# The credit for GpSimd is taken out of the rule that chooses engines during attention

## The chip, the cores and the metric

The kernel runs on one core of a Trainium2 chip. The metric is the device time of one execution in microseconds; lower is better. The core's engines are named as in the profile: PE is TensorE's matmul (PEld its weight load), DVE is VectorE, ACT is ScalarE, POOL is GpSimd, SP is SyncE, which here issues the DMAs.

## What is computed

Two layers of a diffusion backbone over 1024 latent tokens and 256 context tokens, all in float32. Each layer normalises and modulates its input, projects it, and feeds three branches: a gated convolution of width 31, windowed attention, and gated linear attention in chunks of 64. Their gated outputs are concatenated and go through one output projection. The part that matters here is the attention's softmax, cut from the reference:

```python
s_loc = jnp.where(mn, jnp.einsum('bqhgd,bkhd->bhgqk', qn, kn).astype(F32), NEG_INF)
s_ctx = jnp.einsum('bqhgd,bchd->bhgqc', qn, kc).astype(F32)
p = jax.nn.softmax(jnp.concatenate([s_sink, s_ctx, s_loc], axis=-1), axis=-1)
...
return (jnp.einsum('bhgqc,bchd->bqhgd', p_ctx, vc)
        + jnp.einsum('bhgqk,bkhd->bqhgd', p_loc, vn))
```

## The kernel before, in words

**Scheduling.** The program is written by generators ("lanes") that run while the kernel is built. A clock model in the kernel (class `Model`) keeps a clock for each engine and adds a price for every instruction that is written. `loop` always continues the lane of the highest priority whose condition the model holds fulfilled. So the model fixes, before anything runs, the order in which each engine gets its instructions; on the chip each engine works through its queue in that order.

**Choosing an engine.** Small elementwise steps can go to more than one engine. `pick` takes the option that ends first by the model: the later of the engine's clock and PE's clock, plus the price, minus a credit from the table `LEAN`. The table has two entries; the second holds while `self.rsv` is set, that is from the start of a layer's attention (`attn_start`) until the scores of its last block are written (`phase_bc`).

```python
c = self.nc.clock
lean = LEAN[1 if self.rsv else 0]
min(opts, key=lambda o: max(c[o[0]], c["pe"]) + o[1] - lean.get(o[0], 0))[2]()
```

GpSimd is an option in three helpers: `scale` (a tile times one number per row; DVE, POOL or ACT), `sub` (DVE or POOL) and `add` (DVE or POOL). `scale` multiplies the attention's probabilities by the inverse of their sum. `sub` makes the low half of every tensor that `split` cuts into a rounded high half and a rest, for the products in three parts: weights, queries, keys and the input of the output projection. `add` adds the residual behind the output projection. The prices that the model uses for n elements per row in `scale` are these:

```python
self.pick(("dve", 130 + n / 1.92, ...),
          ("pool", 110 + 1.1 * n, ...),
          *([("act", 135 + n / 1.4, ...)] if f == 1.0 else []))
```

**Attention.** A unit is one block of 128 queries with 4 heads; layer 0 has 20 units, layer 1 has 16. For each head `u_score` lets PE write the scores into a pair of PSUM banks (two pairs exist), `u_head` masks them and takes the row maximum in one DVE instruction (shown as CUSTOM_DVE_ANT_0; only then is the bank pair free) and ACT exponentiates them. When the four heads are done, `u_run` takes the reciprocal on DVE, scales four tiles P (640 wide, 512 or 256 in some blocks), and PE transposes them by products with the identity (`idr`); `u_ev` copies each transpose out on ACT or DVE, and `u_pv` multiplies it with the values. At most two units hold P tiles at one time. `kv_prep` and `q_prep` load and split the keys and queries of later blocks.

**What runs beside it.** The output projection (`out_proj`, `out_tiles`, `out_mm`: 128x256 products of WS or H with H or SM) has the lowest priority but the program itself and fills PE between the units. In layer 0 the gate projections and the modulation of layer 1 do so too.

Of the kernel before, what the change touches and what calls it, by code (L numbers as in the profile page):

```python
# [168 lines left out]
class Hybrid:  # L169
# [190 lines left out]
    def pick(self, *opts):  # L360
# [4 lines that stand above are left out]
# [1399 lines left out]
MODN = 2  # L1764
MODG = 1
MDC = 1
LEAN = ({}, dict(pool=800))
XG = 2000
B_GATE = [(6, 0), (7, 0), (6, 1), (7, 1), (6, 2), (7, 2)]

# [85 lines left out]
```

## Time and profile before

| | |
|---|---|
| median of 3 runs | 1326.59 us (1323.63 to 1327.82) |
| the profiled execution, its own time | 1323.65 us |
| its span, first to last instruction | 1321.9 us |
| PE busy | 1254.0 us, 95% |
| DVE, ACT, POOL busy | 838.4, 561.2, 452.9 us |

All times of views below count from the start of the profiled execution's span. Nearly every instruction carries line 43, that of a helper which issues for all engines, so instructions are told apart by their tiles: SM are small working tiles (P among them), tir small columns, ps PSUM banks, H and WS weights and inputs, U the spare region that attention uses for raw queries.

### The profile page before, as it was taken

Reading aid. Unit: us, or ns where it says so; the run is one execution under the profiler, and the core shown is the slowest. Engines: PE = TensorE matmul, PEld = TensorE weight load, DVE = VectorE, ACT = ScalarE, POOL = GpSimd, SP = SyncE. Lnnn points to the kernel's source line nnn. Section 1 sums busy time; section 2 is a strip of 40 time slices with the busy share of each in tenths; the row PEclk is TensorE's granted clock in tenths of the full one; section 3 lists DMA queues with packets and bytes.
Section 4 is the critical chain, followed back from the end, with each engine's and each line's share of the span. In section 5 each row is a group of like instructions: output and inputs, shape, how many; then the busy total and the mean of one; then the engine's idle time right before and its main releaser. Section 6 shows DMA issues by size and latency. Waiting matters only on the chain.

```text
span 1321.9 us, 24553 instructions
## 1 busy us (share of the span) xinstructions
PE 1254.0 (95%) x9518; PEld 1066.9 (81%) x9518; DVE 838.4 (63%) x1571; ACT 561.2 (42%) x1280; POOL 452.9 (34%) x609
## 2 busy tenths in 40 slices
PE   6999988999999999899999899988999999999997
PEld 3668988898887777687899879977888888788897
DVE  5745897884364463465354676898954656766554
ACT  3721341235332565466541561441245246665531
POOL 1410045674122342444230241055571334344410
PEclk9999989999999999999999999999999999999999
DMA  9453113222014323342132541114231112231012
GB/s 330 151 154 105 48 39 85 70 69 85 25 33 131 112 77 100 96 129 89 49 113 88 156 164 57 49 41 108 71 91 37 55 46 81 73 93 50 33 65 81
DMA packets 113237, 116.49 MB, mean 88 GB/s; under 512 B 38464, under 2 KB 81760, under 8 KB 113120
## 3 DMA queue, kind: packets, MB, share of 16 engines
q1 hardware_dynamic: 113120, 114.92, 28.5%
q8 instruction: 75, 1.23, 0.4%
q14 instruction: 42, 0.34, 0.1%
HBM read 95.47 MB, written 19.42 MB: 87 GB/s over the span
## 4 chain that ended last, share of the span: by engine, by line
PE 69%; DVE 8%; POOL 6%; DMA 6%; issue 5%; ACT 4%; SPq 1%; POOLq 0%; DVEq 0%; ACTq 0%
PE ps L43 69%; POOL SM L43 4%; DVE SM L43 3%; ACT SM L43 2%; DVE mix L43 2%; DMA WR<-in_w_out_dram 2%; DVE H L43 2%; DMA WR<-in_w_mod_dram 2%; POOL WR L43 1%; DMA WR<-in_w_in_dram 1%; DVE WS L43 1%; SPq L43 1%; DMA HC<-in_w_mod_dram 1%; ACT H L43 1%; ACT L43 0%
## 5 line engine op out<-in xcount | busy, mean ns | idle before, releaser
L43 PE MATMUL ps<-H,WS 128*128 128x512 f32 x1344 | 339.7, 400 | 2.9 <-DVE stat L43 1.4
L43 PEld LDWEIGHTS ps<-H,WS 128*128 128x128 f32 x1344 | 244.3, 189 | 63.8 <-issue 12.2
L43 PE MATMUL ps<-WS,H 128*128 128x256 f32 x1744 | 254.8, 291 | 0.0
L43 PEld LDWEIGHTS ps<-WS,H 128*128 128x128 f32 x1744 | 230.4, 195 | 10.0 <-issue 9.5
L43 ACT ACTIVATE SM<-ps 128x512 f32<-128x512 f32 (+2 forms) x164 | 82.7, 509 | 343.6 <-PE ps L43 289.3
L43 DVE SCALAR_TENSOR_TENSOR mix<-U,small,mix 128x1295 f32<-128x1295 f32 (+1 forms) x120 | 180.9, 1549 | 0.0
L43 PE MATMUL ps<-idr,SM 128*128 128x128 f32 (+1 forms) x1076 | 150.5, 273 | 26.2 <-POOL SM L43 16.4
L43 PEld LDWEIGHTS ps<-idr,SM 128*128 128x128 f32 (+1 forms) x1076 | 120.0, 142 | 56.0 <-POOL SM L43 22.0
L43 DVE CUSTOM_DVE_ANT_0 SM<-ps,SM,small 128x640 f32<-128x640 f32 (+2 forms) x128 | 102.7, 813 | 60.1 <-PE ps L43 53.5
L43 ACT ACTIVATE SM<-SM,stat 128x641 f32<-128x641 f32 (+2 forms) x144 | 110.7, 769 | 69.5 <-DVE stat L43 47.2
L43 POOL TENSOR_TENSOR tir<-tir,mhalf 128x1 f32<-128x1 f32 (+2 forms) x55 | 47.3, 863 | 199.2 <-DVE tir L43 192.3
L43 POOL TENSOR_TENSOR SM<-SM,SM 128x128 fp32r<-128x128 f32 (+3 forms) x59 | 60.9, 1041 | 158.7 <-ACT SM L43 107.9
L43 PE MATMUL ps<-H,H 128*128 128x256 f32 x592 | 99.0, 287 | 3.7 <-DVE H L43 2.0
L43 ACT ACTIVATE H<-ps 128x512 f32<-128x512 f32 (+1 forms) x129 | 72.7, 596 | 65.2 <-PE ps L43 63.7
L43 POOL TENSOR_SCALAR SM<-SM,tir 128x640 f32<-128x640 f32 (+2 forms) x90 | 75.8, 855 | 44.3 <-DVE tir L43 29.7
L43 PEld LDWEIGHTS ps<-H,H 128*128 128x128 f32 x592 | 83.8, 189 | 5.5 <-DVE H L43 2.2
L43 ACT ACTIVATE SM<-SM 32x128 f32<-32x128 f32 (+3 forms) x194 | 70.3, 369 | 38.3 <-DVE SM L43 30.0
L43 PE MATMUL ps<-SM,SM 128*32 128x128 f32 (+4 forms) x764 | 79.0, 285 | 5.9 <-DMA SM<-vd 3.1
L43 PE MATMUL ps<-H 128*64 128x256 f32 x548 | 72.3, 388 | 0.7 <-ACT ps L43 0.3
L43 POOL TENSOR_TENSOR SM<-SM,WR 128x256 f32<-128x256 f32 (+2 forms) x60 | 61.8, 1036 | 20.0 <-DVE SM L43 13.8
L43 DVE TENSOR_TENSOR WS<-WR,WS 128x512 fp32r<-128x512 f32 x66 | 60.7, 932 | 5.2 <-ACT WS L43 3.6
L43 PEld LDWEIGHTS ps<-SM,SM 128*64 128x64 f32 (+2 forms) x764 | 45.4, 127 | 20.0 <-ACT SM L43 6.1
(151 smaller groups left out, 1989.8 us busy)
## 6 DMA issues: line engine op xcount, KB each, us to landing
WR<-in_w_in_dram SPq DMA_DIRECT2D x80, 256.0 KB, 3.7
WR<-in_w_mod_dram SPq DMA_DIRECT2D x64, 256.0 KB, 3.2
WR<-in_w_out_dram SPq DMA_DIRECT2D x32, 256.0 KB, 3.5
SM<-vd SPq DMA_DIRECT2D x116, 64.0 KB, 2.4
x<-SM SPq DMA_DIRECT2D x20, 256.0 KB, 2.5
SM<-x SPq DMA_DIRECT2D x20, 256.0 KB, 4.3
qd<-SM SPq DMA_DIRECT2D x18, 256.0 KB, 2.2
mix<-in_x_dram SPq DMA_DIRECT2D x8, 512.0 KB, 8.3
```

Source lines behind the costliest of these rows:

```text
L43: r = getattr(self._e, op)(*a, **k)
```

## The change

The credit for GpSimd is removed from the second entry of the table. No other line differs.

```diff
-LEAN = ({}, dict(pool=800))
+LEAN = ({}, {})
```

Since the chosen engine moves the model's clocks, the written order changes with it, from the first scores of layer 0's attention to that layer's end and again in layer 1's attention; what stands ahead of each attention is almost the same. The counts over the whole program: of the 144 scalings of P, POOL had 86, DVE 40 and ACT 18; now POOL has 45, DVE 72 and ACT 27. Of the subtractions and additions 72 go from POOL to DVE. In layer 1, POOL's scalings of P fall from 34 to 26 only.

POOL, layer 0, the eighth unit: its four P tiles (SM_671 to SM_674) before the change, with a weight's low half ahead and a query's behind.

```order
L43 TENSOR_TENSOR H_0_105_495<-WR_707_5091,H_0_105_495 128x512
L43 TENSOR_SCALAR SM_671_4959<-SM_671_4959,tir 128x640
L43 TENSOR_SCALAR SM_672_4960<-SM_672_4960,tir 128x640
L43 TENSOR_SCALAR SM_673_4961<-SM_673_4961,tir 128x640
L43 TENSOR_SCALAR SM_674_4962<-SM_674_4962,tir 128x640
L43 TENSOR_TENSOR SM_719_5176<-U,SM_719_5176 128x4x64
```

DVE at the same unit after the change: its tiles are now SM_701 to SM_704, and ISA is the masking with the maximum.

```order
L43 ISA SM_704_5038,stat<-ps_67,SM_426_3819,small 128x640
L43 ISA stat 128x1
L43 CAST H_1_7_112<-ps_68 128x512
L43 CAST SM_713_5122<-U 128x4x64
L43 CAST H_0_105_495<-WR_712_5102 128x512
L43 TENSOR_TENSOR H_0_105_495<-WR_712_5102,H_0_105_495 128x512
L43 RECIPROCAL tir<-stat 128x4
L43 TENSOR_SCALAR SM_701_5035<-SM_701_5035,tir 128x640
L43 TENSOR_SCALAR SM_702_5036<-SM_702_5036,tir 128x640
L43 TENSOR_SCALAR SM_704_5038<-SM_704_5038,tir 128x640
```

Three of the four scalings now stand in DVE's queue one behind the other, and so does the weight's low half; the fourth is ACT's.

PE in layer 1 after the change, where the ninth unit begins: products of the output projection (ps_71 and ps_70), the transposes of two prepared keys (SM_1589, SM_1591), then the unit's first scores (HC).

```order
L43 MATMUL ps_71<-H_1_106_496,H_1_7_112 128x256 x2
L43 MATMUL ps_71<-H_1_106_496,SM_1580_11523 128x256
L43 MATMUL ps_68<-idr,SM_1589_11673 128x128 x4
L43 MATMUL ps_69<-idr,SM_1591_11683 128x128 x4
L43 MATMUL ps_70<-H_0_105_495,H_1_7_112 128x256 x12
L43 MATMUL ps_66<-HC_494 128x256 x2
L43 MATMUL ps_66<-HC_494 128x128 x2
```

Ahead of these scores 234 products of the output projection stand with no score between them; before the change the most between two scores of one attention was 60. The keys wait for working tiles, which the output projection holds. From the ninth unit's first score to the sixteenth's, PE had 634 products before, 288 of them of the output projection; now it has 486, with 156. DVE's own instructions there number 88 before and 89 now.

## Rows read from the trace of the kernel before

**Rows 1.** The page: the span, and busy time of each engine over it.

```profile
span 1321.9 us, 24553 instructions
...
PE 1254.0 (95%) x9518; PEld 1066.9 (81%) x9518; DVE 838.4 (63%) x1571; ACT 561.2 (42%) x1280; POOL 452.9 (34%) x609
```

**Rows 2.** Both attentions: length; busy PE, PEld, DVE, ACT, POOL; clock, DMA share, GB/s.

```profile
433.00:683.00 250.00, 240.69 (x1821) 189.38 (x1820) 131.02 (x312) 143.52 (x322) 94.09 (x174) 1.00 0.30 91
...
1073.00:1278.00 205.00, 201.32 (x1553) 172.44 (x1552) 133.06 (x288) 121.56 (x259) 85.02 (x144) 1.00 0.21 65
```

**Rows 3.** PE's waits in 433:683, by what ended them: us in total, times, longest.

```profile
PE ps L43 <- DVE H L43: 3.4, 3, 2.0
PE ps L43 <- POOL H L43: 1.7, 2, 1.0
PE ps L43 <- DVE stat L43: 0.9, 2, 0.5
PE ps L43 <- DVE SM L43: 0.8, 1, 0.8
PE ps L43 <- POOL SM L43: 0.7, 2, 0.4
```

**Rows 4.** The same in 1073:1278.

```profile
PE ps L43 <- DVE stat L43: 1.8, 3, 0.9
PE ps L43 <- POOL SM L43: 1.0, 3, 0.3
PE ps L43 <- DVE tir L43: 0.6, 1, 0.6
```

**Rows 5.** POOL's groups by shape, whole run: busy, mean ns, idle before.

```profile
L43 POOL TENSOR_SCALAR SM<-SM,tir 128x640 f32<-128x640 f32 x54 | 49.9, 937 | 15.8 <-DVE tir L43 15.7
...
L43 POOL TENSOR_TENSOR WS<-WR,WS 128x512 fp32r<-128x512 f32 x22 | 31.4, 1431 | 71.5 <-ACT WS L43 47.8 <-DVE WS L43 19.8 <-PE ps L43 3.6
```

**Rows 6.** DVE's groups by shape, whole run.

```profile
L43 DVE CUSTOM_DVE_ANT_0 SM<-ps,SM,small 128x640 f32<-128x640 f32 x96 | 83.6, 879 | 47.2 <-PE ps L43 44.1 <-POOL SM L43 1.5 <-issue 1.5
L43 DVE TENSOR_TENSOR WS<-WR,WS 128x512 fp32r<-128x512 f32 x66 | 60.7, 932 | 5.2 <-ACT WS L43 3.6
...
L43 DVE TENSOR_SCALAR SM<-SM,tir 128x640 f32<-128x640 f32 x26 | 21.7, 867 | 0.4
...
L43 DVE TENSOR_SCALAR H<-ps 128x512 f32<-128x512 f32 x24 | 16.4, 686 | 11.9 <-PE ps L43 10.5 <-ACT SM L43 1.4
L43 DVE TENSOR_TENSOR mix<-ps,mix 128x256 f32<-128x256 f32 x36 | 15.2, 422 | 42.7 <-PE ps L43 41.6 <-issue 0.9
...
L43 DVE TENSOR_TENSOR SM<-U,SM 128x256 fp32r<-128x256 f32 x6 | 3.7, 616 | 3.2 <-ACT SM L43 3.2
```

**Rows 7.** Timeline in 538:562: POOL and DVE (start, us, what, idle before).

```profile
542.20 3.13 POOL L43 TENSOR_SCALAR SM<-SM,tir 128x640 f32<-128x640 f32 x4 [0.47 <-DVE tir L43]
...
548.06 0.55 DVE L43 TENSOR_SCALAR SM<-SM,tir 128x640 f32<-128x640 f32 x1
549.77 0.56 DVE L43 CAST H<-WR 128x512 fp32r<-128x512 f32 x1 [1.16 <-DMA WR<-in_w_out_dram]
```

**Rows 8.** Timeline of PE in 542.0:550.5.

```profile
544.61 0.33 PE L43 MATMUL ps<-idr,SM 128*128 128x128 f32 x1 [0.28 <-POOL SM L43]
545.38 1.41 PE L43 MATMUL ps<-idr,SM 128*128 128x128 f32 x9 [0.44 <-POOL SM L43]
...
550.39 0.39 PE L43 MATMUL ps<-H,H 128*128 128x256 f32 x1 [2.03 <-DVE H L43]
```

**Rows 9.** Timeline in 1107:1112: DVE and POOL scale at the same time.

```profile
1108.48 1.58 DVE L43 TENSOR_SCALAR SM<-SM,tir 128x640 f32<-128x640 f32 x2
...
1108.55 2.69 POOL L43 TENSOR_SCALAR SM<-SM,tir 128x640 f32<-128x640 f32 x2 [2.66 <-DVE tir L43]
```

**Rows 10.** Busy time by stretch: ninth to sixteenth unit of layer 1, then output projection alone.

```profile
1176.00:1260.00 84.00, 83.45 (x689) 74.39 (x686) 54.90 (x117) 50.12 (x110) 35.41 (x63) 1.00 0.17 56
...
1280.00:1305.00 25.00, 25.00 (x215) 25.00 (x214) 14.41 (x27) 3.62 (x10) 1.21 (x2) 1.00 0.22 74
```

## Prediction

> **What bounds the kernel now.** I read the page first: PE is busy for 1254.0 us of a span of 1321.9 [rows 1], so no other engine can give back more than the 68 us in which PE stands still. The change is silent outside attention, so I cut the two attentions out next, layer 0 from 433 to 683 and layer 1 from 1073 to 1278 [rows 2]. The reader is to see three things there: the granted clock is 1.00, the upper level (2.4 GHz), in both; PE is busy for 240.69 of 250 and for 201.32 of 205 us, so it idles for 9.3 and 3.7 us, 13.0 together; and DVE is busy for 131.0 (52%) and 133.1 us (65%), POOL for 94.1 and 85.0. Thirteen us is therefore the most that any choice of engines can win in attention if PE's work stays the same, while a loss has no such bound.
>
> Then I asked who ends PE's idle time. In layer 0 DVE ends 3.4 + 0.9 + 0.8 = 5.1 us of the listed waits and POOL 1.7 + 0.7 = 2.4 [rows 3]; in layer 1 DVE 1.8 + 0.6 = 2.4 and POOL 1.0 [rows 4]. One of DVE's waits isn't its own: PE stood for 2.03 us before 550.39 for a weight half of DVE [rows 8], and DVE's rounding of weights there had itself waited 1.16 us for a DMA [rows 7]. I take that 2.0 off, which leaves 3.1 us in layer 0. What the change aims at is also visible: at 542.20 POOL scales four tiles of P in a row, 3.13 us [rows 7], and PE's transposes wait twice for them, 0.28 and 0.44 us [rows 8].
>
> **What the change moves, and what each part costs.** By the written order POOL loses 41 scalings of P and 72 subtractions and additions. DVE gains 32 of the scalings and all 72 others; ACT gains 9 scalings. The other moves (a few roundings and evictions between ACT and DVE) about cancel in the attentions, and I price them at nothing. PE's own work and the DMAs stay the same but for their order.
>
> *Time added to DVE.* A scaling of 640 takes 0.55 us on DVE when POOL doesn't scale beside it [rows 7] and 0.867 on average [rows 6]. The 72 others are 30 of 128 columns, 17 of 256 and 25 of 512. For the 47 narrow ones I take bounds of 0.42 (a two-input product of 256) and 0.62 (a subtraction of 256 as it now stands), for the wide ones 0.69 (a one-input copy of 512) and 0.93 (a weight's low half) [rows 6]. Low: 32 x 0.55 + 47 x 0.42 + 25 x 0.69 = 54.6 us. High: 32 x 0.87 + 47 x 0.62 + 25 x 0.93 = 80.2 us. I take 55, the low end, since POOL's work about halves: what leaves it is, as an estimate from [rows 5, 7], 41 x 0.78 + 47 x 0.8 (taken like a scaling) + 25 x 1.43 = 105 of 179 us at most. Of the moved instructions 62 are layer 0's (28 scalings, 34 others) and 42 layer 1's (4 and 38): 33 and 22 us.
>
> *(a) PE's waits for DVE grow.* DVE works in order, and the instruction that frees a pair of score banks (0.879 us) [rows 6] now stands behind up to four scalings and the low halves. I let these waits grow as DVE's busy time over its idle time. Layer 0: 131/119 = 1.10 becomes 164/86 = 1.91, a factor of 1.73, so 3.1 us grow by 2.3. Layer 1: 133/72 = 1.85 becomes 155/50 = 3.1, a factor of 1.68, so 2.4 us grow by 1.6. Sum +3.9. At the high price (48 and 32 us) the factors are 2.3 and 2.2 and the sum is +6.9. From below the bound is no growth, or even that these 5.5 us vanish, if DVE is slowed by POOL more than by its own queue.
>
> *(b) PE's waits for POOL shrink.* They are 2.4 + 1.0 = 3.4 us. POOL keeps 45 scalings and about half of its work, so I take half: -1.7, between 0 and -3.4.
>
> *(c) The cover in the second half of layer 1 gets thin.* Before the ninth unit's scores the new order has a run of 234 products of the output projection. They cost 25.00/215 = 0.116 us each [rows 10], some 27 us in which attention stands, because its keys wait for working tiles. From the ninth unit's first score to the sixteenth's, 148 of 634 products are gone, 17 us of PE's work. Now that stretch takes 84 us, with PE busy for 83.45 and DVE for 54.9 [rows 10]; with the same 54.9 us of DVE in 84 - 17 = 67 us, DVE is busy for 82% of it. Unit by unit it is tighter. The thirteenth unit's stretch now has 58 products on PE, 6.7 us at 0.116, and on DVE three scalings, four maxima, four copies of transposes and two products: 3 x 0.55 + 4 x 0.88 + 4 x 0.69 + 2 x 0.42 = 8.8 us [rows 6, 7]. Counted in this way DVE has more than PE in three of the seven units, by 1.5, 2.2 and 1.5 us; before the change in three, by 0.6, 0.1 and 1.1. The difference is 3.4. I take +3, between 0 (the lateness is caught up in the next unit) and +7 (all DVE prices at their averages).
>
> Sum: 3.9 - 1.7 + 3.0 = +5.2 us. Against the profiled execution's own 1323.65 us (span 1321.9 and 1.75 around it) that is 1328.9. That execution lies 2.9 us under the median of the runs, 1326.59; on the median the same 5.2 us give **1332 us**, and that is my forecast. Its own range is 1331 to 1341: above it the high ends of (a) and (c) without (b), +13.9. Changes below about 0.3% (4 us) can't be told from none by a measurement of this kernel, so "same" means 1322.6 to 1330.6.
>
> **The rivals.** *Faster: DVE and POOL stand in each other's way, and the change parts them.* At 1108.48 DVE scales two tiles in 1.58 us while POOL scales two in 2.69 [rows 9]; by themselves such pairs take 1.10 and 1.57 (2 x 0.55, and half of 3.13) [rows 7]. Side by side they cost 0.5 and 1.1 us more. If this lengthening is what makes PE wait for DVE, then taking half of POOL's work away ends all waits for POOL (-3.4) and half of those for DVE (-2.7): -6.1, 1320.5 us. It decides if DVE's busy time in the two attentions grows by less than about 20 us instead of 55, since then (a) falls to about +1 and (b) outweighs it. For it: a DVE scaling's mean is 0.867, not 0.55. Against it: DVE's longest instructions read PSUM and don't show this (0.879 on average over 96), and 5.1 us of listed waits in layer 0 are behind DVE, 2.4 behind POOL. The Trainium skill, "SBUF — State Buffer", section "SBUF: two separate sides", has a rule that speaks for this rival: DVE in a two-port mode or with two inputs from SBUF and GpSimd hold a shared port pair in turn, each for a whole instruction. By that rule, the trace agrees for scalings side by side; it doesn't tell how much of it reaches PE.
>
> *No change: the cover holds.* PE idles for only 13 us of 455 in attention; a late DVE result may mostly meet PE while it is behind its order anyway. Then (a) and (c) stay under +3 together, and the time is 1326.6 + 3 - 1.7 = 1328 us. Layer 1 speaks for it too: only 8 scalings of P leave POOL there, so the change hardly does what it says, and what it does besides, with the subtractions, is spread over 205 us.
>
> **How the numbers follow.** Slower by over 0.3% by (a) and (c): 0.48. The same: 0.29. Faster by the parted engines: 0.23. The range for 8 in 10 reaches from the rival's 1320 to the high ends' 1341; about 1 in 10 is left out on each side.
>
> **What would show it.** Right: DVE busy in layer 0's attention up from 131 to about 164 us and in layer 1's from 133 to about 155, POOL's about halved; PE's waits ended by DVE up to about 5 and 4 us, those by POOL down to half; in layer 1 some 27 us of output projection with no score, and behind it PE waiting unit after unit for DVE's maxima and copies. Wrong: DVE's mean scaling falls to 0.6 us and its busy time grows by less than 20 us, and PE's idle time in the attentions falls below 13 us; or it stays at 13 and nothing moves. The forecast also fails if the run of 234 products ends later on the chip than written, so that the last units stand bare at the end of the program; that would cost more than +7.

## The result and the profile after

The change made the kernel slower: 1333.88 us (median of 5 runs, 1331.63 to 1336.22) against 1327.82 us of the kernel before beside it (5 runs, 1323.63 to 1331.30). The medians differ by 6.1 us. The ratio on record, which is not that of these two medians, is 1.0063 with a 95% interval of 1.0042 to 1.0084: 8.4 us on 1327.82, and from 5.6 to 11.2 by the interval. The text below goes by the ratios.

The page of the kernel after, span and busy time, to be laid beside [rows 1]:

```profile
span 1332.0 us, 24546 instructions
...
PE 1257.9 (94%) x9518; PEld 1069.6 (80%) x9518; DVE 879.7 (66%) x1686; ACT 561.4 (42%) x1276; POOL 368.2 (28%) x498
```

The span grew by 10.1 us. PE's busy time grew by 3.9 of them although it has the same 9518 products; the other 6.2 are time in which PE stands still. DVE gained 41 us and POOL lost 85. The two attentions after, as in [rows 2]:

```profile
433.00:688.00 255.00, 246.38 (x1858) 195.76 (x1857) 152.85 (x362) 144.61 (x322) 45.77 (x113) 0.99 0.29 87
...
1073.00:1295.00 222.00, 212.51 (x1610) 180.91 (x1609) 151.36 (x323) 125.12 (x267) 54.59 (x103) 0.98 0.20 64
```

In layer 0 PE idles for 8.6 us, before for 9.3; in layer 1 for 9.5, before for 3.7. The granted clock is no longer 1.00. PE's waits, first 433 to 688, then 1073 to 1295, against [rows 3, 4]:

```profile
PE ps L43 <- POOL SM L43: 2.2, 2, 2.0
PE ps L43 <- DVE H L43: 2.2, 2, 1.8
...
PE ps L43 <- DVE SM L43: 0.7, 2, 0.6
PE ps L43 <- DVE stat L43: 0.7, 1, 0.7
```

```profile
PE ps L43 <- DVE stat L43: 7.1, 4, 5.4
PE ps L43 <- DVE SM L43: 1.8, 3, 0.9
PE ps L43 <- DVE H L43: 0.2, 1, 0.2
```

In layer 0 the waits behind DVE fell from 5.1 us (5.7 with one of 0.6 that [rows 3] leave out) to 3.6. In layer 1 they rose from 2.4 (2.6 with one of 0.2 that [rows 4] leave out) to 9.1, and one of them alone has 5.35. That one can be followed in the timeline of DVE, then POOL, then PE in layer 1's third and fourth unit (start, us, what, idle before):

```profile
1104.39 0.43 DVE L43 CAST WS<-WR 128x512 fp32r<-128x512 f32 x1 [0.50 <-PE ps L43]
1104.85 0.69 DVE L43 TENSOR_TENSOR WS<-WR,WS 128x512 fp32r<-128x512 f32 x1
1105.46 0.42 DVE L43 CAST WS<-WR 128x512 fp32r<-128x512 f32 x1
1106.34 1.50 DVE L43 TENSOR_TENSOR WS<-WR,WS 128x512 fp32r<-128x512 f32 x1 [0.46 <-ACT WS L43]
1107.76 1.66 DVE L43 TENSOR_TENSOR H<-mix,H 128x512 fp32r<-128x512 f32 x1
1109.34 0.87 DVE L43 CUSTOM_DVE_ANT_0 SM<-ps,SM,small 128x640 f32<-128x640 f32 x1
```

```profile
1106.02 1.27 POOL L43 TENSOR_TENSOR WS<-WR,WS 128x512 fp32r<-128x512 f32 x1 [5.98 <-issue]
1107.42 1.45 POOL L43 TENSOR_TENSOR SM<-mix,H 128x512 fp32r<-128x512 f32 x1
```

```profile
1102.80 1.55 PE L43 MATMUL ps<-H,WS 128*128 128x512 f32 x6
1104.19 0.74 PE L43 MATMUL ps<-HC,H 128*128 128x256 f32 x4
1110.28 2.93 PE L43 MATMUL ps<-H,WS 128*128 128x512 f32 x6 [5.35 <-DVE stat L43]
1113.00 1.27 PE L43 MATMUL ps<-HC,H 128*128 128x256 f32 x4
```

The scores written at 1104.19 fill a pair of banks, and PE's next products, the gate projection's, go into the same pair. They wait for the maximum at 1109.34, and ahead of it DVE has five instructions of weights and input. Two of these run beside POOL's: a low half that takes 0.69 us alone takes 1.50 and 1.66, and each ends some 0.55 us after POOL's instruction did (1107.84 after 1107.29, 1109.42 after 1108.87). Then six gate products take 2.93 us, which had taken 1.55 ahead of the wait. The busy time and clock of these stretches:

```profile
1090.00:1100.00 10.00, 10.00 (x72) 8.35 (x68) 8.63 (x19) 6.26 (x16) 3.41 (x8) 1.00 0.65 208
1100.00:1108.00 8.00, 4.92 (x32) 3.30 (x30) 5.55 (x11) 4.23 (x9) 1.88 (x3) 1.00 0.12 28
1108.20:1115.00 6.80, 4.72 (x15) 4.14 (x16) 5.46 (x10) 2.16 (x4) 0.67 (x1) 0.50 0.21 71
```

While PE waits, the granted clock falls from 1.00 to 0.50, from the upper of its two levels (2.4 GHz) to the lower (1.2 GHz), and PE starts again at the lower one. The prediction had no term for that.

### The profile page after: what moved, and what is told of

Its sections match the earlier page's. It is cut to its first block, busy times and chain, and to the rows that moved or that the text cites. A ratio compares the mean times of both kernels' runs of the same rounds, so it can differ in the third digit from the quotient of the medians.

```text
span 1332.0 us, 24546 instructions
## 1 busy us (share of the span) xinstructions
PE 1257.9 (94%) x9518; PEld 1069.6 (80%) x9518; DVE 879.7 (66%) x1686; ACT 561.4 (42%) x1276; POOL 368.2 (28%) x498
## 4 chain that ended last, share of the span: by engine, by line
PE 72%; DVE 8%; DMA 6%; POOL 5%; issue 4%; ACT 3%; SPq 1%; POOLq 0%; DVEq 0%; ACTq 0%
PE ps L43 72%; POOL SM L43 4%; DVE SM L43 3%; DVE mix L43 2%; ACT SM L43 2%; DVE H L43 2%; DMA WR<-in_w_mod_dram 2%; DMA WR<-in_w_in_dram 1%; POOL WR L43 1%; SPq L43 1%; DMA HC<-in_w_mod_dram 1%; DVE WS L43 1%; DMA WR<-in_w_out_dram 0%; DMA SM<-x 0%; ACT L43 0%
## 5 line engine op out<-in xcount | busy, mean ns | idle before, releaser
L43 ACT ACTIVATE SM<-ps 128x512 f32<-128x512 f32 (+3 forms) x163 | 82.2, 509 | 341.4 <-PE ps L43 282.6
L43 ACT ACTIVATE H<-ps 128x512 f32<-128x512 f32 (+1 forms) x121 | 68.8, 597 | 72.8 <-PE ps L43 69.3
L43 ACT ACTIVATE SM<-SM 32x128 f32<-32x128 f32 (+4 forms) x200 | 72.1, 367 | 41.8 <-DVE SM L43 29.3
L43 POOL TENSOR_TENSOR SM<-SM,SM 128x512 f32<-128x512 f32 (+2 forms) x33 | 46.6, 1415 | 131.6 <-ACT SM L43 112.3
L43 POOL TENSOR_SCALAR SM<-SM,tir 128x640 f32<-128x640 f32 (+2 forms) x51 | 42.1, 837 | 86.4 <-DVE tir L43 78.0
L43 POOL COPY SM<-small 128x1 f32<-128x1 f32 x144 | 26.9, 233 | 124.0 <-PE ps L43 104.2
```

The lines of the kernel that those rows point to most:

```text
L43: r = getattr(self._e, op)(*a, **k)
```

## The experiments

Names used below. **Theory Q** is the prediction's: DVE's load makes PE wait (terms a and b). **Theory O**: the written order that comes out of the other choices costs the time, whichever engine does the work. Within it, **T** blames the run of 234 products and the thin cover behind it (term c), **S** the single wait of 5.35 us. **L**: DVE and POOL stand in each other's way. **C**: a long wait of PE costs its length and then a slower clock. Each ratio is to runs of the kernel before on the same chip, 1325.5 to 1326.2 us.

**1 and 2. Work and order apart.** `pick` takes both choices, with the credit and without; the instruction goes to one engine, while the clock model prices it on the other (`as_if`), so that the written order is that of the other kernel. Shown is the first experiment; the second swaps the indices 0 and 1.

```diff
-min(opts, key=lambda o: max(c[o[0]], c["pe"]) + o[1] - lean.get(o[0], 0))[2]()
+by = [min(opts, key=lambda o: max(c[o[0]], c["pe"]) + o[1] - x.get(o[0], 0))
+      for x in (lean, {})]
...
+if by[0] is not by[1]:
+    self.nc.as_if = (by[0][0], op)
+by[1][2]()
+self.nc.as_if = None
```

> The order of PE is word for word that of before; every instruction that only the credit gave to POOL is issued to DVE or ACT (DVE has 137 more instructions than before, where the change has 115 more; POOL 164 fewer, the change 111 fewer), and the kernel's clock model goes on pricing them on POOL. Theory Q (the load of DVE's queue, terms a and b of the prediction): 3 to 6 us over before, about 1330 to 1334, with more waits of PE behind DVE in both attentions. Theory O (the written order: the run of 234 products of the output projection and the thin cover behind it, term c): within 2 us of before, about 1326 to 1330. Rival L (DVE and POOL stand in each other's way): 3 to 6 us faster than before.

Measured: 1.0017 (1.0003 to 1.0031), +2.3 us. In the order of before, DVE has more instructions than in the change (1708 against 1686) and is busy for nearly as long (874.7 us against 879.7), and most of the loss is gone. Rival L, which said 3 to 6 us faster, missed.

> The other way round: the order of PE is word for word that of the change, with the run of 234 products in layer 1, but the instructions that the credit would give to POOL are issued to POOL (DVE has 57 instructions fewer than before, POOL 86 more). Theory Q: the loss is gone, 1325 to 1330, PE's wait of 5.35 us near 1110 gone too. Theory O: as slow as the change, 1332 to 1336, with long waits of PE behind the run of 234. Rival L: slower than the change, over 1336, since POOL is busy beside DVE again.

Measured: 1.0204 (1.0176 to 1.0233), +27 us. This is the slowest of all, and the wait near 1110 is there again with 5.57 us. Theory Q falls as the main cause. So does the plain form of O: the order isn't simply worth its loss, it is much worse still when POOL does the work for which the order was not planned. Rival L had said "over 1336" here and came out right, but it had missed in the first experiment, so it isn't the cause by itself. In the first eight units of layer 1 PE now waits 5.3 us for POOL's tiles:

```profile
PE ps L43 <- DVE stat L43: 6.5, 2, 5.6
PE ps L43 <- POOL SM L43: 5.3, 11, 0.9
```

**3 and 4. One layer each.**

```diff
-self.rsv = True
+self.rsv, self.lay = True, l
...
-lean = LEAN[1 if self.rsv else 0]
+lean = LEAN[1 if self.rsv and self.lay == 0 else 0]
```

> The credit holds in layer 0's attention only; layer 1's attention has the change, with the same run of 234 products. By the prediction's terms layer 1 has 4.1 of the 5.2 us: a +1.6, b -0.5, c +3.0, so 1330 to 1334. If the loss lay in layer 0's heavier queue of DVE alone (28 of the 32 scalings that DVE gains are there): 1326 to 1329.

Measured: 1.0068 (1.0047 to 1.0090), +9.0 us: layer 1 has the whole loss.

> The credit holds in layer 1's attention only; layer 0's attention has the change. By the prediction's terms layer 0 costs a +2.3 and b -1.2, about +1: 1327 to 1330. If the loss is layer 0's queue of DVE: 1331 to 1335. If it is the new falls of the granted clock behind waits in layer 0 (two of 3.41 us at half speed in the trace of the change, at most 1.7 us each) and nothing else: 1330 to 1331.

Measured: 0.9971 (0.9956 to 0.9986), -3.8 us. This version, with the change in layer 0 and the credit in layer 1, is faster than both kernels. Layer 0's part of the change is no loss.

**5 to 8. Which feature of layer 1's order?** Two kernels keep the change and alter what one lane of layer 1 asks of the working tiles; two keep layer 0's change and give layer 1 a credit of another size.

```diff
-yield (self.need("SM", 2 - early, 1), ...
+yield (self.need("SM", 2 - early, 4 if l else 1), ...
```

> The change, and in layer 1 the output projection starts a block only when four working tiles stay free behind it, not one. The run of 234 products is gone (the longest between two scores of layer 1 is 48), 492 products stand behind the last score instead of 282; DVE's queue ahead of PE's wait at 1110 keeps its four weight halves and loses one of the input's. Theory T (the thin cover behind the run costs most of the 9 us that the third experiment found in layer 1): 1321 to 1327. Theory S (the single wait of 5.35 us at 1110 and the slower clock behind it cost most): 1329 to 1333. Theory Q (DVE's load, which is the same as in the change): 1330 to 1334.

Measured: 1.0115 (1.0083 to 1.0146), +15 us, above all three ranges. The run is gone and the kernel is slower than the change: theory T isn't borne out, though what this order loses elsewhere may hide a gain. The single wait is still there, with 3.76 us, and the six products behind it take 2.93:

```profile
1110.97 2.93 PE L43 MATMUL ps<-H,WS 128*128 128x512 f32 x6 [3.76 <-DVE stat L43]
```

New waits came in the last eight units, most of them behind POOL's tiles:

```profile
PE ps L43 <- POOL SM L43: 3.5, 5, 1.6
PE ps L43 <- DVE SM L43: 1.7, 2, 0.9
```

```diff
-yield self.need("SM", 2, PK), ...
+yield self.need("SM", 2, 0 if l else PK), ...
...
```

> The change, and in layer 1 the preparation of keys and queries asks for no spare working tile beside its own. The run of 234 products becomes one of 90, and the five instructions of weights and input that stood ahead of the maximum at PE's wait of 5.35 us become two. DVE has 1689 instructions, the change 1688. Theories T and S alike: 1320 to 1326, as the fourth experiment or a little under it. Theory Q: 1330 to 1334. Told apart from each other by the fifth and seventh.

Measured: 1.0053 (1.0033 to 1.0073). A miss for T and S alike, since the run was down to 90 products and the burst ahead of the maximum from five instructions to two. In place of the one wait there are several in the first eight units:

```profile
PE ps L43 <- DVE stat L43: 4.7, 5, 2.5
PE ps L43 <- POOL SM L43: 1.4, 1, 1.4
```

```diff
-lean = LEAN[1 if self.rsv else 0]
+lean = LEAN[1 + self.lay if self.rsv else 0]
...
-LEAN = ({}, dict(pool=800))
+LEAN = ({}, dict(pool=0), dict(pool=1000))
```

> Layer 0 has the change; in layer 1 the credit is 1000, above that of before, so that POOL has more work there than before. The written order nevertheless has a run of 234 products of the output projection ahead of the ninth unit, and 258 behind the last score; at the place of the wait of 5.35 us only three short instructions stand ahead of the maximum. Theory T: 1329 to 1335. Theory S: 1321 to 1326. Theory Q (layer 1's load on DVE is as light as before): 1321 to 1325.

Measured: 1.0060 (1.0039 to 1.0082). A larger credit, with POOL busier in layer 1's attention than before (98.9 us against 85.0) and with the run of 234, loses as much as none. T and O had this right, Q and S (1321 to 1326) had not; but it came by another way than T's: the longest of PE's waits is 1.06 us, the granted clock in layer 1's attention stays at 1.00, and there are many waits, in the first eight units above all. So an order can lose as much without any long wait.

> Layer 0 has the change; in layer 1 the credit is 400. DVE has 1674 instructions, nearly the change's 1688, but the written order has no run over 42 products and leaves 462 behind the last score. Theories T and S: 1320 to 1325. Theory Q: the loss of layer 1 is nearly whole, 1328 to 1333.

Measured: 1.0005 (0.9989 to 1.0021). With nearly the change's work on DVE the time is that of before; 1 us over what T and S expected, 2 us under Q's range.

**9. The wait at 1110 alone.** Of all subtractions two, the last two of DVE's five instructions above, go to POOL; the model prices them on DVE, so nothing else moves.

```diff
+if self.nsub in TO_POOL:
+    nc.as_if = "dve", "tensor_tensor"
+    nc.gpsimd.tensor_tensor(o, a, b, op=ALU.subtract)
+    nc.as_if = None
+    return
...
+TO_POOL = (244, 246)
```

> The change, and only two of the five instructions that stand on DVE ahead of the maximum at PE's wait of 5.35 us (a weight's low half, 1.50 us, and an input's, 1.66 us) are issued to POOL; the order of every engine is otherwise word for word the change's. Theory S (that wait and the slower clock behind it are most of layer 1's loss): the wait falls by about 3 us to about 2, the stretch at half speed of 6.83 us behind it gets shorter or goes, and the time falls by 3 to 6 us under the change, to 1328 to 1331. If PE only waits a little later for POOL instead, or what is behind gives nothing back: within 2 us of the change, 1332 to 1336.

Measured: 1.0026 (1.0009 to 1.0043), and 1328.57 us against the change's 1333.88. Two instructions of 24546 bring back 0.0063 - 0.0026 = 0.0037, about 4.9 us; the two intervals together leave 1 to 8. PE at this place, where everything stands 2.9 us later in the span:

```profile
1105.67 1.55 PE L43 MATMUL ps<-H,WS 128*128 128x512 f32 x6
1107.07 0.74 PE L43 MATMUL ps<-HC,H 128*128 128x256 f32 x4
1109.62 2.08 PE L43 MATMUL ps<-H,WS 128*128 128x512 f32 x6 [1.81 <-DVE stat L43]
```

The wait fell from 5.35 to 1.81, by 3.5 us, and the six products behind it from 2.93 to 2.08. The slower clock didn't go; its stretch got shorter (first line). Below it, from layer 1's first maximum to the end, stand the kernel after and this one:

```profile
1110.60:1114.00 3.40, 3.40 (x14) 3.17 (x14) 3.40 (x3) 1.74 (x4) 3.40 (x3) 0.51 0.55 186
...
1073.20:1332.00 258.80, 241.11 (x1851) 209.36 (x1849) 168.65 (x354) 129.47 (x279) 56.23 (x106) 0.98 0.20 65
...
1075.90:1331.10 255.20, 240.91 (x1852) 209.11 (x1850) 168.39 (x352) 129.47 (x279) 59.11 (x108) 0.98 0.20 66
```

By these traces 3.6 us are back, 3.4 of them idle time. So theory S holds for a part of the loss: 3.6 of the 10.0 us by which this stretch had grown, or 4.9 of 8.4 by the ratios. What the remaining wait of 1.81 us and the slower products behind it cost wasn't measured.

**10. A credit near the fourth's**, `dict(pool=0), dict(pool=700)`.

> Layer 0 has the change; in layer 1 the credit is 700 instead of the 800 of the fourth experiment. The written order is nearly the same (longest run of the output projection 48 products, not 60; 372 behind the last score in both), and seven instructions fewer stand on DVE. Theory O (the order sets the time): as the fourth experiment, 1320 to 1325. Any smooth effect of the credit's size (800: 1323, 400: 1326, none: 1334): 1323 to 1325 as well; if single orders are luck from 700 to 800 too, it can lie anywhere from 1322 to 1332.

Measured: 0.9993 (0.9972 to 1.0015). As expected of a nearly equal order, but a smooth effect of the credit's size would give the same. It also says how much the fourth's gain is worth: layer 0 is the same in both and layer 1 nearly, and the two ratios stand for -0.9 and -3.8 us, so layer 0's gain is about 1 to 4 us; by the tenth's interval it could be nothing.

**11 and 12. What a wait costs.** The kernel before, with the masking instruction repeated ahead of the real one (the same result is written again). The model doesn't see it, so the order is that of before.

```diff
+for _ in range(LATE.get((u.key, h), 0)):
+    nc.nc.vector.tensor_tensor_reduce(o, a, mk, -0.125, ...)
 nc.vector.tensor_tensor_reduce(o, a, mk, -0.125, ...)
...
+LATE = {("1.1.0", 3): 6}
```

> The kernel before, with one maximum of layer 1's third unit (fourth head) written seven times instead of once: DVE has six instructions of about 0.88 us more at one place, nothing else differs and the clock model doesn't see them. Theory C (a long wait of PE costs its length and then a slower clock): PE waits about 5.5 us there, the granted clock is at half for some us behind it, and the time grows by 6 to 9 us. The wait alone: 4 to 6 us. If PE's lateness is made up behind it: under 3 us.

Measured: 1.0060 (1.0037 to 1.0084), +8.0 us. PE waits 6.09 us, 0.52 at the same place before (first line), and the rows show the same as at the change's wait: a score group of 0.85 us takes 1.44, six gate products 2.68, at a clock of 0.50.

```profile
1106.47 0.85 PE L43 MATMUL ps<-HC,H 128*128 128x256 f32 x4 [0.52 <-DVE stat L43]
...
1105.16 0.60 PE L43 MATMUL ps<-SM,H 128*64 128x256 f32 x4
1111.86 1.44 PE L43 MATMUL ps<-HC,H 128*128 128x256 f32 x4 [6.09 <-DVE stat L43]
1113.09 2.68 PE L43 MATMUL ps<-H,WS 128*128 128x512 f32 x6
```

```profile
1090.00:1100.00 10.00, 10.00 (x63) 7.86 (x59) 6.14 (x15) 6.22 (x14) 4.29 (x9) 1.00 0.51 162
...
1109.00:1115.00 6.00, 3.15 (x9) 2.76 (x10) 4.55 (x14) 1.50 (x3) 0.48 (x1) 0.50 0.00 0
```

> The kernel before with the same added work on DVE, but spread: one more copy of the maximum at the fourth head of six units in a row (second to seventh unit of layer 1). Theory C: PE's waits stay near or under 1 us each, the granted clock stays at its upper level, and the time grows by 1 to 4 us, clearly less than in the eleventh experiment. If only the amount of DVE's work on the path counts, both grow alike, by 4 to 6 us.

Measured: 1.0028 (1.0013 to 1.0043), +3.7 us. The same added work in six portions costs about half as much; the longest new wait is 1.45 us and the clock in layer 1's attention stays at 1.00:

```profile
1109.67 0.85 PE L43 MATMUL ps<-HC,H 128*128 128x256 f32 x4 [1.45 <-DVE stat L43]
...
1075.50:1282.60 207.10, 200.71 (x1545) 171.59 (x1544) 138.38 (x297) 121.92 (x259) 85.14 (x144) 1.00 0.21 64
```

How much of the difference is the clock's can be read from layer 1's first maximum to the end, in the kernel before, the eleventh and the twelfth:

```profile
1073.10:1321.90 248.80, 237.21 (x1856) 208.13 (x1854) 154.30 (x326) 126.62 (x273) 87.32 (x148) 0.99 0.21 67
...
1073.10:1328.50 255.40, 238.53 (x1855) 209.61 (x1853) 160.02 (x338) 126.92 (x273) 87.48 (x148) 0.98 0.20 66
...
1075.50:1327.30 251.80, 237.55 (x1856) 208.24 (x1854) 160.46 (x338) 126.99 (x273) 87.45 (x148) 0.99 0.21 67
```

The single burst makes the stretch 6.6 us longer: 5.3 are idle time and 1.3 longer products. The six portions make it 3.0 longer: 2.7 and 0.3. Theory C holds in kind, but the clock's share is the small one. Of the 3.6 us between the two, 2.6 are idle time, since about half of the spread work doesn't make PE wait at all, and 1.0 is longer products.

PE's idle time in layer 1 (the length of each stretch less its busy time; from the first maximum to the ninth unit's, from there to the last unit's last product, and behind it):

| kernel | units 1 to 8 | units 9 to 16 | behind | ratio |
|---|---|---|---|---|
| before | 3.1 | 0.6 | 7.9 | 1 |
| after | 7.1 | 2.4 | 8.2 | 1.0063 |
| 1, work moved, order kept | 4.3 | 0.6 | 7.9 | 1.0017 |
| 2, order moved, work kept | 13.6 | 5.0 | 7.9 | 1.0204 |
| 3, change in layer 1 alone | 7.1 | 2.5 | 7.9 | 1.0068 |
| 4, change in layer 0 alone | 3.3 | 0.6 | 8.2 | 0.9971 |
| 5, four tiles kept free | 6.5 | 7.3 | 7.9 | 1.0115 |
| 6, no reserve | 6.9 | 2.8 | 8.2 | 1.0053 |
| 7, credit 1000 | 8.8 | 3.5 | 8.2 | 1.0060 |
| 8, credit 400 | 3.6 | 2.9 | 8.3 | 1.0005 |
| 9, two to POOL | 3.7 | 2.4 | 8.2 | 1.0026 |
| 10, credit 700 | 3.3 | 0.9 | 8.2 | 0.9993 |

Kernels 1, 4 and 10, whose order in layer 1 is that of before or nearly so, idle least there; the ratio follows the idle time and not DVE's load.

## Why the prediction was right, and where it wasn't

**The sum.** 1332.0 us was forecast, with 1331 to 1341 as the likeliest case's range; 1333.88 came. The direction and about the size are right, but two errors of opposite sign stand behind it, so that the size is in part luck. By the prediction's terms layer 0 had +1.1 and layer 1 +4.1 us; the fourth and third experiments measured -3.8 (the tenth: -0.9) and +9.0.

**Time added to DVE**, taken at 33 and 22 us, was 22 and 18: too high. The moved instructions aren't free, but those that DVE had already got shorter:

```profile
L43 DVE TENSOR_TENSOR WS<-WR,WS 128x512 fp32r<-128x512 f32 x72 | 62.9, 883 | 6.4 <-ACT WS L43 4.5
L43 DVE TENSOR_SCALAR SM<-SM,tir 128x640 f32<-128x640 f32 x42 | 25.7, 660 | 0.3
...
L43 DVE TENSOR_TENSOR SM<-U,SM 128x256 fp32r<-128x256 f32 x14 | 7.1, 506 | 1.8 <-ACT SM L43 1.4
```

The scaling fell from 867 ns to 660, and in the first experiment, where POOL is busy for 321.8 us instead of 368.2, to 586; the weights' low half fell from 932 to 883, the narrow one from 616 to 506 [rows 6]. These durations agree with the exclusive port lock that the faster rival rested on (the Trainium skill, "SBUF — State Buffer", section "SBUF: two separate sides"), and so do 1106.34 and 1107.76, where DVE's instruction ends only after POOL's has.

**(a), PE's waits for DVE**, is the step that failed. In layer 0 +2.3 was forecast and the waits fell from 5.1 to 3.6. In layer 1 +1.6 was forecast and they rose by 6.5, of which one wait has 5.35; without it the rise would be 1.2. Letting waits grow as DVE's busy over its idle time treats the queue as an average. What decided was where in the queue one burst stood, and that pair of banks for which PE had nothing else to do. With the order kept, the first experiment costs +2.3 us, where (a) and (b) together said +2.2, but that agreement is luck: in its trace layer 0's attention, which should have half of it, is no longer than before, and from layer 1's first maximum to the end 1.2 us are idle time and 2.2 longer products.

**(b), PE's waits for POOL**, fell as forecast in layer 1 (1.0 to none), but hardly in layer 0 (2.4 to 2.2, since one new wait has 2.0).

**(c), thin cover**, was +3 in a range of 0 to +7. Idle time in units nine to sixteen rose from 0.6 to 2.4 us, +1.8. The run of 234 products came as written. Nothing shows that the time hangs on it: without it (5) the kernel is slower and idles for 7.3 us in these units, with a run of 90 (6) it idles for 2.8, and in the ninth the whole run stands and part of the loss is gone. The seventh, with the run and as slow as the change, fits (c), but its idle time lies mostly ahead of the run's end, in units one to eight.

**Missing: the clock.** From layer 1's first maximum to the end the kernel before took 248.8 us, the one after 258.8. Of these 10.0 us 6.1 are idle time. The other 3.9 are longer products, at about the same number of them (1856 and 1851). At 1110.28 and 1113.00 alone the difference is (2.93 - 1.55) + (1.27 - 0.74) = 1.9; what the rest comes from isn't known. The clock can't be all of it: in the ninth experiment the stretch at half speed is shorter and the busy time is still 240.9 us against 241.1.

**The rivals.** "Faster" was to decide if DVE's time grew by less than 20 us; it grew by 40. The lengthening is real, by the durations above, and layer 0's part of the change gained some 1 to 4 us, but that the one is the reason of the other isn't shown: with the engines parted and the order kept (1), layer 0's attention takes as long as before (249.3 us, 249.4 before). "No change" lost to layer 1, where the prediction counted only 8 scalings that move and so held the change for small; the order changed there all the same.

**What stays open.** The ninth experiment accounts for about 4.9 of the 8.4 us, with 1 to 8 as its range. The remaining 3.5 and the layer 0 gain together mean, as an estimate, that some 4 to 8 us stand elsewhere in layer 1 or in what is left of the single wait; by the ninth's trace layer 1 is still 6.4 us longer than before (255.2 against 248.8). Which feature of an order loses them isn't shown: four other orders of layer 1 (5 to 8) lose 0 to 15 us in different places.

## What to carry to other kernels

Where a planner's constant chooses engines, it also rewrites the order; measure the two apart, by issuing to one engine while the model prices the other, and one part of the program at a time, before crediting or blaming the engine. A constant that was found together with one order isn't a smooth dial: with layer 0 changed, 400, 700 and 800 in layer 1 gave 0.9971 to 1.0005 of the time before, 0 and 1000 gave 1.006. In a forecast look for the one place where PE's next product needs a bank that a queue with a burst ahead of it must free, instead of scaling all waits by a load.

## What was not expected of the hardware

A wait of PE cost more than its length. Behind the waits of 5.35 and 6.09 us PE worked at the lower clock level (0.50, 1.2 GHz) for some us, and six products took 2.93 and 2.68 us instead of 1.55. With six spread waits of at most 1.45 us the clock in layer 1's attention stayed at 1.00, and the same added work cost 3.7 instead of 8.0 us; most of that difference is idle time and about 1 us the clock, as worked out above. The wait's length alone doesn't tell whether the clock falls: behind the ninth experiment's 1.81 us it fell to 0.51, while in the eighth a longer wait (first line) left it at 1.00:

```profile
1195.01 0.66 PE L43 MATMUL ps<-idr,SM 128*128 128x128 f32 x4 [2.29 <-DVE H L43]
...
1193.00:1203.00 10.00, 7.99 (x62) 5.89 (x64) 8.98 (x19) 5.80 (x14) 4.17 (x7) 1.00 0.17 61
```

Not every stretch at half speed belongs to the change: in the first 433 us, which are the same in all kernels here, the trace's clock records show 6.8 to 13.7 us of them from one execution to the next.
